# Keys stored in runs for three dilations, strided queries copied by GpSimd, rotary tables made in place

## The chip, the core and the metric

The kernel runs on one core of a Trainium2 chip. The metric is the device time of one execution in microseconds, the median of several runs. The engines run side by side, each through its own queue in order: TensorE (PE; its weight loads are PEld), VectorE (DVE), ScalarE (ACT), GpSimd (POOL), and SyncE (SP), which here only issues DMAs.

## What is computed

A decoder layer on 2048 tokens of 1024 channels: an adaLN-modulated RMS norm, one input projection, then two mixers side by side, a gated linear recurrence (512 channels) and an attention of 8 heads of 64 with rotary queries and keys, and an output projection. What matters here is the attention. It is done three times, with (window, dilation) of (128, 1), (512, 4) and (2048, 16), and the three results are mixed by their softmax denominators:

```python
def dilated_attention(q, k, v, window, dilation):
    L = S // dilation
    blk = window // dilation                       # 128 in all three
    ...                                            # token l * dilation + r goes to residue r, place l
    scores = einsum('bhrnqd,bhrnkd->bhrnqk', qb, kc)   # a block of 128 queries, its own and the previous 128 keys
    scores = where(valid, scores, NEG_INF)
    ...
outs, lses = zip(*[dilated_attention(qh, kh, vh, w, d) for (w, d) in DILATED_PATTERNS])
wts = softmax(stack(lses), axis=0)
att = einsum('pbhs,pbhsd->bhsd', wts, stack(outs))
```

All is float32. The kernel splits each operand of a matmul into a high and a low part and adds three products.

## The kernel before

**First stage.** The tokens go in four chunks of 512. Per chunk: load x (`load_x`), normalise, transpose, modulate into a high and a low part of h (`prep_h`, L301), then the projections. `qk` (L376) multiplies four 128x512 tiles from PSUM by the cosine and sine tables and stores rotated queries and keys, split in two, to DRAM (L395). The tables of a chunk come from `trig` (L238): a DMA broadcasts 512 positions to all partitions into a turn buffer (`half_t` or `rot_t`, which `qk` and `gb` use as well), VectorE reduces the angles, ScalarE takes sines, VectorE finishes into `cos_t`. `v` (L398) scales a value tile by ScalarE, and SP stores it (L406). Weights come through `weights` (L317): DMA, a cast by ScalarE, the low part by GpSimd (L344). The chunks run in two halves (0, 1 and 2, 3); `load(2)` and `load(3)` hold the `trig` of their chunk. In this stage a planner orders the instructions of each engine from its own costs.

**Attention** (`attend`, L1097). Here PE, DVE, ACT and POOL keep the written order; SP's order stays the planner's. Four head pairs, one head in each half of the partitions. `load_pair` brings q and k (high and low, `qs`, `kh`, `kl`), `load_values` the values, one DMA per pattern and chunk. A pair has 19 groups in the order of `SEQUENCE` (L32): 0 is dilation 1, 1 dilation 4, 2 dilation 16. A group has two units of 128 queries by 256 keys, or four units by 128 keys (dilation 16, and the first chunk of dilation 4). Per group: `scores` (L654) issues, for each unit, three products for each of the two heads, the queries as weights and the keys as moving operand, both read with the step of the dilation (`slice(r0, r1, 4)`); VectorE adds the mask and takes the minimum (L670), ScalarE the exponentials (L678); four or five steps later (a step is one head of a group, 38 a pair) `transposed` (L681) and `values` (L696) follow; `evacuate` (L711) writes the result back in token order.

**Mixing the patterns.** Events are counted in steps (`after`, L733). The statistics of a chunk go through DRAM and back (`turn_stats`, `pass_stats`, L755 to L763); `shares` (L765) is called for chunks 0 to 2 at the end of the pair and for chunk 3 some 20 steps into the next, and stores the weights of the patterns (L787). `spread` (L792) reads them back as W, broadcast over 64 partitions, for chunk n of the pair, 7 steps apart; three steps later `combine` (L801) gives GpSimd six operations of 128x512 (L805 to L808), and six steps after that `split_y` (L811) has a copy by VectorE (L815) and a subtraction by GpSimd (L816). So most of this work of a pair falls into the next pair.

**Last stage** (`project`, L1124): the output projection, block by block, the recurrent part ahead of the attention part, the closing norm and the store.

## Time and profile before

| | us |
|---|---|
| three runs | 1185.92, 1184.37, 1180.71 |
| median | 1184.37 |
| the profiled execution | 1180.56 |
| its span, first to last instruction | 1178.8 |

| engine | busy us | share of the span | instructions |
|---|---|---|---|
| PE | 1096.3 | 93% | 6645 |
| DVE | 758.4 | 64% | 1655 |
| ACT | 612.6 | 52% | 1512 |
| POOL | 457.3 | 39% | 297 |

[...] How the views are read: a windows row gives the stretch, its length, the busy us of PE, PEld, DVE, ACT and POOL with their counts, then the granted clock, the DMA engines' busy share and GB/s. A timeline row gives start, duration, engine, line, operation, out<-in and count, and in brackets how long the engine had been idle before it and what it waited for; neighbours of one kind are merged, so matmuls that overlap show a longer time together than they take of the engine, and the distance to the next start is what they cost. A wait row says who waited for whom. DMA-issuing instructions don't count as busy.

### The profile page before, as it was taken

To read this page: it belongs to the slowest core of one execution; us is meant where nothing else is said; L and a number is where in the kernel's file an instruction comes from. 1 tells how busy PE (TensorE), PEld (TensorE's weight loads), DVE (VectorE), ACT (ScalarE), POOL (GpSimd) and SP (SyncE) were. 2 spreads that over 40 slices of the span, in tenths; PEclk is the share of its full clock that TensorE was granted. 3 is DMA by queue.
4 is the path that set the end of the run, shared out by engine and by line. 5 is a ranking of instruction groups with operands and counts; after the bars stand their busy time and mean duration, and the time that the engine had idled before them with its cause. 6 is when DMAs were issued, how large, how long until landed. Compare 5 with 4: busy or idle time off the path is not lost.

```text
span 1178.8 us, 18472 instructions
## 1 busy us (share of the span) xinstructions
PE 1096.3 (93%) x6645; PEld 899.0 (76%) x6645; DVE 758.4 (64%) x1655; ACT 612.6 (52%) x1512; POOL 457.3 (39%) x297
## 2 busy tenths in 40 slices
PE   5868999869989999999999999999999998999996
PEld 2546888768967778888898888878777876778885
DVE  4766497677555645879565266687597783355556
ACT  5544353447547223654545377767678674223332
POOL 1434434234143553436234170083361563742222
PEclk9988999999999999999999999989999989999998
DMA  9533335152253344427222724858659447976654
GB/s 338 191 116 131 116 119 169 60 180 90 85 147 125 110 141 135 124 91 196 82 90 77 227 77 98 179 135 221 164 124 236 127 146 147 269 231 215 186 152 143
DMA packets 164859, 176.49 MB, mean 150 GB/s; under 512 B 25168, under 2 KB 119840, under 8 KB 164768
## 3 DMA queue, kind: packets, MB, share of 16 engines
q1 hardware_dynamic: 164768, 175.32, 51.9%
q8 instruction: 52, 0.85, 0.3%
q14 instruction: 39, 0.32, 0.1%
HBM read 124.49 MB, written 50.79 MB: 149 GB/s over the span
## 4 chain that ended last, share of the span: by engine, by line
PE 52%; DMA 18%; DVE 12%; POOL 7%; issue 5%; ACT 4%; SPq 2%; DVEq 0%; POOLq 0%; ACTq 0%
PE sp L665 5%; DMA st_s<-stat 3%; PE pt L688 3%; DMA wgate<-in_w_ada 3%; DMA W<-f_s 2%; PE pvo L705 2%; PE pv L369 2%; PE pv L370 2%; PE pv L371 2%; PE pmixa L909 2%; POOL W L805 2%; PE pmixb L927 2%; PE pmixa L907 2%; PE pgb L358 2%; PE pgb L357 2%
## 5 line engine op out<-in xcount | busy, mean ns | idle before, releaser
L344 POOL TENSOR_TENSOR wl<-wst,wh 128x1024 fp32r<-128x1024 f32 (+2 forms) x72 | 138.5, 1945 | 203.1 <-ACT wh L342 203.1
L670 DVE CUSTOM_DVE_ANT_0 pm<-sp,table 128x256 f32<-128x256 f32 (+1 forms) x384 | 119.2, 360 | 48.3 <-PE sp L665 42.9
L665 PE MATMUL sp<-kh,qs 64*128 64x256 f32 (+1 forms) x768 | 131.9, 388 | 8.9 <-DVE S L670 5.2
L805 POOL TENSOR_TENSOR W<-W,o 128x512 f32<-128x512 f32 x48 | 60.7, 1294 | 151.0 <-DMA W<-f_s 151.0
L665 PEld LDWEIGHTS sp<-kh,qs 64*128 64x128 f32 x768 | 100.8, 274 | 24.0 <-issue 12.4
L688 PE MATMUL pt<-table,pm 128*128 128x128 f32 x600 | 88.8, 294 | 2.7 <-ACT pT L693 1.5
L705 PE MATMUL pvo<-pT,vt 128*64 128x128 f32 (+1 forms) x1072 | 87.6, 306 | 0.0
L342 ACT CAST wh<-wst 128x1024 fp32r<-128x1024 f32 (+2 forms) x72 | 51.8, 761 | 56.3 <-DMA wst<-in_w_in 26.6
L688 PEld LDWEIGHTS pt<-table,pm 128*128 128x128 f32 x600 | 69.4, 148 | 15.1 <-issue 3.0
L369 PE MATMUL pv<-wh,hh 128*128 128x256 f32 x256 | 72.8, 284 | 7.6 <-ACT vr L404 4.4
L705 PEld LDWEIGHTS pvo<-pT,vt 128*64 128x64 f32 x1072 | 63.4, 144 | 19.2 <-issue 14.4
L370 PE MATMUL pv<-wl,hh 128*128 128x256 f32 x256 | 72.7, 284 | 3.6 <-POOL wl L344 3.6
L952 POOL TENSOR_TENSOR mix<-mix,xt 128x1024 f32<-128x1024 f32 x15 | 36.6, 2441 | 100.1 <-DVE mix L951 60.1
L665 PE MATMUL sp<-kl,qs 64*128 64x256 f32 (+1 forms) x384 | 75.4, 366 | 0.0
L678 ACT ACTIVATE pm<-pm,stat 128x256 f32<-128x256 f32 (+1 forms) x128 | 60.2, 474 | 25.5 <-DVE stat L670 25.5
L371 PE MATMUL pv<-wh,hl 128*128 128x256 f32 x256 | 72.3, 282 | 0.0
L678 ACT ACTIVATE pm<-pm,turn 128x256 f32<-128x256 f32 (+1 forms) x128 | 62.8, 495 | 16.3 <-DVE turn L670 16.3
L357 PE MATMUL pa<-hl,wh 128*128 128x512 f32 x128 | 52.7, 412 | 17.0 <-DVE hl L313 14.7
L691 DVE COPY pT<-pt 128x512 f32<-128x512 f32 (+1 forms) x96 | 63.7, 679 | 0.8 <-PE pt L688 0.5
L665 PEld LDWEIGHTS sp<-kl,qs 64*128 64x128 f32 x384 | 57.8, 277 | 0.0
L437 DVE SCALAR_TENSOR_TENSOR xc<-xr,cols,xc 128x512 f32<-128x512 f32 x48 | 55.5, 1156 | 0.8
L369 PEld LDWEIGHTS pv<-wh,hh 128*128 128x128 f32 x256 | 49.0, 191 | 8.8 <-ACT vr L404 5.1
(275 smaller groups left out, 3131.8 us busy)
## 6 DMA issues: line engine op xcount, KB each, us to landing
wst<-in_w_in SPq DMA_DIRECT2D x32, 512.0 KB
W<-f_s SPq DMA_DIRECT2D x32, 384.0 KB
x_t<-in_x SPq DMA_DIRECT2D x16, 512.0 KB
wada<-in_w_ada SPq DMA_DIRECT2D x16, 512.0 KB
wst<-in_w_in SPq DMA_DIRECT2D x32, 256.0 KB
vt<-v_s SPq DMA_DIRECT2D x32, 256.0 KB
yat<-y_s SPq DMA_DIRECT2D x32, 256.0 KB
yb_s<-yb SPq DMA_DIRECT2D x16, 512.0 KB
```

What stands on the lines that cost most here:

```text
L344: nc.gpsimd.tensor_tensor(lo, i, hi.bitcast(F32), ALU.subtract)
L357: nc.tensor.matmul(o, lhsT=wh[:, k, sl], rhs=hl[:, k, :], start=False, stop=False)
L369: nc.tensor.matmul(o[:, 0:256], lhsT=hh[:, k, sl], rhs=wh[:, k, :], start=k == 0, stop=False)
L370: nc.tensor.matmul(o[:, 0:256], lhsT=hh[:, k, sl], rhs=wl[:, k, :], start=False, stop=False)
L371: nc.tensor.matmul(o[:, 0:256], lhsT=hl[:, k, sl], rhs=wh[:, k, :], start=False, stop=k == KC - 1)
L665: nc.tensor.matmul(self.sp[h][:, o:o + n], lhsT=x[rows, q], rhs=y[rows, k], start=j == 0, stop=j == 2)
L670: v.tensor_tensor_reduce(out=pm[:, o:o + n], in0=sp[:, o:o + n], in1=self.mask[:, 256 - n:256], scale=-0.125, scalar=3e38, op0=ALU.add, op ...
L678: nc.scalar.activation(pm[:, o:o + n], pm[:, o:o + n], AF.Exp, bias=self.stat(ctx, s, b), scale=-1.0, accum_out=self.stat(ctx, 2 + s, b))
L688: nc.tensor.transpose(pt[:, k * P:(k + 1) * P], pm[:, k * P:(k + 1) * P], self.ident)
L691: nc.vector.tensor_copy(pT[:, 0:tot], pt[:, 0:tot])
L705: self.mark = nc.tensor.matmul(self.bank[p][64 * s:64 * s + 64, o:o + w], lhsT=ctx["vt"][p, b][:, s], rhs=ctx["pT"][:, c:c + w], start=fir ...
L805: e.tensor_tensor(W[:, p], W[:, p], self.o.pop((pr, p, n)), ALU.mult)
```

## The change

- Keys: within a chunk of 512, token 16 i + r is stored at place 32 r + i. `qk` does this in its four products for K, reading PSUM and the tables with a step of 16 elements and writing in a row. The scores then read the keys of any dilation in runs (8 elements for dilation 1, 32 for 4 and 16). A dilation-1 unit of 256 keys that spans two chunks becomes two matmuls of 128 columns per product.
- The masks of dilation 1 and 4 get the same order (`masks`, two VectorE copies), and so do the values: their loads for dilation 1 and 4 are four DMAs instead of one.
- Queries of dilation 4 and 16 are copied side by side by GpSimd (`queries`: two copies of 128x512 per chunk or four units, 16 a pair), issued two groups ahead (`AHEADQ`), into two buffers that take the place of `cos_t`. Dilation-1 queries are read as before.
- `trig` works in the table itself, and its position DMA writes there: for chunks 0 and 1 before the modulation's weights are loaded, for 2 and 3 right before `trig`.
- The value stores are issued by ScalarE instead of SP.
- The six operations of `combine` are given to GpSimd as four one step later and two another step later.

```diff
+AHEADQ = 2
...
+    def masks(self, pool):
+        self.masked = [pool.tile([P, 2 * P], F32, name=f"mask{r}") for r in (16, 4)] + [self.mask]
+        for r, m in zip((16, 4), self.masked):
+            self.nc.vector.tensor_copy(m.rearrange("p (two r i) -> p two r i", two=2, r=r),
+                                       self.mask.rearrange("p (two i r) -> p two r i", two=2, r=r))
...
+    def load_positions(self, c):
+        pi = self.cos_t[:, 2 * (c % 2) + 1, :].bitcast(I32)
+        self.nc.sync.dma_start(pi, self.io["positions"][:, c * CH:(c + 1) * CH].to_broadcast([P, CH]))
     def trig(self, c):
-        rot = self.turn()
-        pi = rot[:, 0, :].bitcast(I32)
-        nc.sync.dma_start(pi, self.io["positions"][:, c * CH:(c + 1) * CH].to_broadcast([P, CH]))
...
+        cos, sin = (self.cos_t[:, 2 * (c % 2) + n, :] for n in range(2))
+        v.tensor_copy(sin, sin.bitcast(I32))
...
     def qk(...)
+        def times(to, x, y):
+            if which == "k":
+                to = to.rearrange("p (r i) -> p r i", r=16)
+                x, y = (t.rearrange("p (i r) -> p r i", r=16) for t in (x, y))
+            nc.vector.tensor_tensor(to, x, y, ALU.mult)
...
     def v(...)
-            nc.sync.dma_start(self.v_s[r0:r0 + P, 4 * quad:4 * quad + 4, :], vr)
+            nc.scalar.dma_start(self.v_s[r0:r0 + P, 4 * quad:4 * quad + 4, :], vr)
...
     def load_values(...)
+        elif p == 1:
+            for m in range(4):
+                self.nc.sync.dma_start(flat[32 * m:32 * m + 32],
+                                       vs.rearrange("(i m r) e -> m i r e", m=4, r=4)[m])
+        else:
+            for b in range(4):
+                self.nc.sync.dma_start(flat[:, b], vs[P * b:P * b + P].rearrange("(i r) e -> r i e", r=16))
...
+    def keys(x, p, blocks):
+        c, j = divmod(blocks[0], 4)
+        if p == 2:
+            return [(x.rearrange("p (c r i) -> p r c i", c=4, r=16)[:, blocks[0]], 0, P)]
+        if p == 1:
+            n = len(blocks)
+            x = x[:, c * CH:(c + n) * CH].rearrange("p (c m r i) -> p r c m i", c=n, m=4, r=4)
+            return [(x[:, j], 0, n * P)]
+        x = [x[:, c * CH:c * CH + CH].rearrange("p (r b i) -> p b r i", r=16, b=4) for c in (c, c + (j == 3)) if c < 4]
+        if len(blocks) == 1 or j < 3:
+            n = len(blocks)
+            return [(x[0][:, j:j + n], 0, n * P)]
+        return [(x[0][:, 3], 0, P), (x[1][:, 0], P, P)]
+    def queries(self, p, n):
+        self.copies = (self.copies + 1) % 2
+        q = self.qc[self.copies]
+        x = self.qs.rearrange("p k (i r) -> p k r i", r=16)[:, :, 4 * n:4 * n + 4] if p == 2 else (
+            self.qs[:, :, n * CH:n * CH + CH].rearrange("p k (i r) -> p k r i", r=4))
+        for k in range(2):
+            self.nc.gpsimd.tensor_copy(q[:, k], x[:, k].bitcast(F32))
+        return q
...
     in source(), attention()
+                    copy_queries(pr, i + AHEADQ)
...
     def combine(...)
+        for i in range(3):
+            self.after(i, lambda some=ops[2 * i:2 * i + 2]: [e.tensor_tensor(*op) for op in some])
         self.after(SPLIT, lambda: self.split_y(cb, gb, pr, n))
```

## Rows read from the trace of the kernel before

**Rows 1.** Windows by stage: the first stage, then the four head pairs of the attention.

```profile
0.00:667.70 667.70, 612.39 (x3013) 498.13 (x3013) 429.04 (x557) 322.65 (x533) 251.68 (x152) 0.97 0.42 134
667.70:736.70 69.00, 68.56 (x651) 57.97 (x650) 47.61 (x218) 52.61 (x204) 26.20 (x18) 0.95 0.46 122
736.70:814.90 78.20, 75.51 (x709) 63.45 (x708) 58.72 (x244) 56.70 (x215) 35.26 (x28) 0.93 0.76 174
814.90:893.40 78.50, 74.67 (x709) 62.91 (x708) 59.58 (x244) 56.59 (x215) 35.14 (x28) 0.96 0.70 165
893.40:973.60 80.20, 75.58 (x710) 63.16 (x710) 61.49 (x248) 56.98 (x214) 35.18 (x28) 0.94 0.59 163
```

**Rows 2.** Timeline, VectorE and TensorE: stands in the first stage.

```profile
93.07 0.43 DVE L245 CAST half_t<-half_t 128x512 f32<-128x512 int32 x1 [12.21 <-DMA half_t<-in_positions]
...
94.15 0.80 PE L357 MATMUL pa<-hl,wh 128*128 128x512 f32 x1 [11.74 <-DVE hl L313]
...
218.27 0.43 DVE L245 CAST rot_t<-rot_t 128x512 f32<-128x512 int32 x1 [10.84 <-DMA rot_t<-in_positions]
...
346.66 0.43 DVE L245 CAST half_t<-half_t 128x512 f32<-128x512 int32 x1 [3.92 <-DMA half_t<-in_positions]
```

**Rows 3.** Windows: two stretches of the first stage.

```profile
200.00:270.00 70.00, 57.15 (x312) 48.87 (x311) 48.69 (x60) 34.09 (x55) 22.47 (x12) 0.93 0.36 113
340.00:370.00 30.00, 22.83 (x112) 18.48 (x112) 19.24 (x28) 15.27 (x21) 6.68 (x4) 0.89 0.25 76
```

**Rows 4.** Waits, ScalarE's and SP's: us in total, times, longest.

```profile
ACT vr L404 <- DMA v_s<-vr: 24.1, 6, 8.5
...
SPq L763 <- DMA st_s<-stat: 69.2, 14, 8.8
```

**Rows 5.** Timeline, TensorE: scores of dilation 16, 4 and 1, each with what follows.

```profile
781.02 0.48 PE L665 MATMUL sp<-kh,qs 64*128 64x128 f32 x2
...
783.81 1.09 PE L688 MATMUL pt<-table,pm 128*128 128x128 f32 x8
...
785.86 0.61 PE L665 MATMUL sp<-kh,qs 64*128 64x256 f32 x2
...
787.58 1.09 PE L688 MATMUL pt<-table,pm 128*128 128x128 f32 x8
...
801.26 0.39 PE L665 MATMUL sp<-kh,qs 64*128 64x256 f32 x2
...
802.16 1.09 PE L688 MATMUL pt<-table,pm 128*128 128x128 f32 x8
```

**Rows 6.** Timeline, TensorE: the first 128-key scores of dilation 1.

```profile
667.90 0.27 PE L665 MATMUL sp<-kl,qs 64*128 64x128 f32 x2
668.01 0.44 PE L665 MATMUL sp<-kh,qs 64*128 64x128 f32 x4
```

**Rows 7.** Single lines of the kernel: duration in ns, minimum, median, maximum.

```profile
L855 POOL CAST wo<-wo_st x6: 609/610/1038, 676.5 to 698.7; 128x512 fp32r<-128x512 f32 x4, 128x1024 fp32r<-128x1024 f32 x2
...
L730 DVE COPY o<-pvo x24: 673/1055/1154, 682.6 to 966.0; 128x512 f32<-128x512 f32 x24
...
L890 DVE TENSOR_REDUCE ysq<-fsq x16: 1018/1078/1097, 1013.2 to 1159.2; 128x128 f32<-128x512 f32 x16
...
L781 DVE TENSOR_TENSOR sd<-sw,S x8: 234/249/1245, 743.4 to 985.5; 96x96 f32<-96x96 f32 x4, 32x96 f32<-32x96 f32 x4
...
L406 SPq DMA_DIRECT2D v_s<-vr x32: 319/320/564, 252.3 to 625.6; - x32
```

**Rows 8.** Timeline, SP's queue: two loads of W in the third head pair.

```profile
833.62 1.26 SPq L796 DMA_DIRECT2D W<-f_s  x2
```

**Rows 9.** Timeline, GpSimd and VectorE: the first weighted sum of that pair.

```profile
843.41 3.74 POOL L805 TENSOR_TENSOR W<-W,o 128x512 f32<-128x512 f32 x3 [31.24 <-DMA W<-f_s]
...
849.80 1.26 POOL L808 TENSOR_TENSOR gbt<-W,gbt 128x512 f32<-128x512 f32 x1
...
851.10 0.43 DVE L815 CAST yb<-gbt 128x512 fp32r<-128x512 f32 x1 [7.35 <-POOL gbt L808]
```

More of the change, by code (lines that the diff above doesn't have):

```diff
@@ L588, in attention, with copy_queries @@
             values_of(0, 1, n)
+        order = [list(self.groups(p)) for p in range(3)]
+        order = [(p, order[p][SEQUENCE[:i].count(p)]) for i, p in enumerate(SEQUENCE)]
+        opens = [p and g[2] for p, g in order]
+        copies = {}
+        def copy_queries(pr, i):
+            if i >= len(order):
+                pr, i = pr + 1, i - len(order)
+            if pr < 4 and opens[i]:
+                p, n = order[i][0], order[i][1][4]
+                copies[pr, p, n] = self.queries(p, n)
         def source():
+            for i in range(AHEADQ):
+                copy_queries(0, i)
             for pr in range(4):
@@ L594, in source @@
                 stat = [turn, cb.tile([P, 4, 16], F32, name="stat1"), S[:, 2]]
-                groups = [self.groups(p) for p in range(3)]
                 left = [SEQUENCE.count(p) for p in range(3)]
-                for i, p in enumerate(SEQUENCE):
-                    g = next(groups[p])
+                for i, (p, g) in enumerate(order):
                     left[p] -= 1
                     n = g[4]
+                    copy_queries(pr, i + AHEADQ)
                     for s in range(2):
-                        yield {"pr": pr, "p": p, "s": s, "g": g, "vt": vts[pr], "stat": stat[p], "S": S}
+                        yield {"pr": pr, "p": p, "s": s, "g": g, "vt": vts[pr], "stat": stat[p], "S": S,
+                               "q": copies.get((pr, p, n))}
                     if pr < 3:
@@ L660, in scores @@
             self.sp = [ps.tile([P, 512], F32, name="sp", tag="mm") for _ in range(2)]
-            for b, q, k, n, o in units:
-                for j, (x, y) in enumerate(((self.qh, self.kh), (self.qh, self.kl), (self.ql, self.kh))):
-                    for h in range(2):
-                        rows = slice(64 * h, 64 * h + 64)
-                        nc.tensor.matmul(self.sp[h][:, o:o + n], lhsT=x[rows, q], rhs=y[rows, k],
-                                         start=j == 0, stop=j == 2)
+            terms = (0, self.kh), (0, self.kl), (1, self.kh)
+            for b, blocks, n, o in units:
+                heads = [slice(64 * h, 64 * h + 64) for h in range(2)]
+                qs = [[ctx["q"][rows, x, b % 4] if p else self.qs[rows, x, P * b:P * b + P] for x in range(2)]
+                      for rows in heads]
+                ks = [[self.keys(y[rows], p, blocks) for _, y in terms] for rows in heads]
+                for part, (_, at, w) in enumerate(ks[0][0]):
+                    for j, (x, _) in enumerate(terms):
+                        for h in range(2):
+                            nc.tensor.matmul(self.sp[h][:, o + at:o + at + w], lhsT=qs[h][x], rhs=ks[h][j][part][0],
+                                             start=j == 0, stop=j == 2)
         sp = self.sp[s]
         pm = wk.tile([P, 512], F32, name="pm", bufs=PMB)
-        for b, q, k, n, o in units:
-            v.tensor_tensor_reduce(out=pm[:, o:o + n], in0=sp[:, o:o + n], in1=self.mask[:, 256 - n:256],
+        for b, _, n, o in units:
+            v.tensor_tensor_reduce(out=pm[:, o:o + n], in0=sp[:, o:o + n], in1=self.masked[p][:, 256 - n:256],
                                    scale=-0.125, scalar=3e38, op0=ALU.add, op1=ALU.min, accum_out=self.stat(ctx, s, b))
@@ L676, in exponentials @@
         s, pm = ctx["s"], ctx["pm"]
[L677 removed]
+        for b, _, n, o in ctx["g"][0]:
             nc.scalar.activation(pm[:, o:o + n], pm[:, o:o + n], AF.Exp, bias=self.stat(ctx, s, b), scale=-1.0,
@@ L1026, in run @@
                     ws = [h1p.tile([P, 4, 2, 512], F32, name="wada", tag=t) for t in ("s1h", "s1l")]
+                    for c in range(2):
+                        self.load_positions(c)
                     self.ada_half(ws, reca, "ri", ps, ld, 0)
@@ L1104, in attend @@
             ps = Banks((psm, 2), (psa, 2))
-            qs = sh.tile([P, 2, T], F32R, name="qs", tag="t1")
-            self.qh, self.ql = (qs[:, s] for s in range(2))
+            self.qs = sh.tile([P, 2, T], F32R, name="qs", tag="t1")
+            qc = sh.tile([P, 2, 2, 4, P], F32R, name="qc", tag="t0")
+            self.qc, self.copies = [qc[:, n] for n in range(2)], 0
             self.kh, self.kl = (sh.tile([P, T], F32R, name=n, tag=t) for n, t in (("kh", "t3"), ("kl", "t4")))
```

64 lines of the change are left out of this document (29 added, 35 removed).

## Prediction

> **What bounds the kernel now.** I read the stages first. Before the first score the core spends 667.7 us, in which TensorE is busy 612.4; the four head pairs of the attention take 69.0, 78.2, 78.5 and 80.2 us, TensorE busy in 68.6, 75.5, 74.7 and 75.6 of them [rows 1]. (The borders are the first score of each pair.) So TensorE sets the pace nearly everywhere, and a gain needs either less time per matmul or the removal of one of its stands. VectorE (59 to 61 us a pair) and ScalarE (57) are not far behind, GpSimd (35) is [rows 1].
>
> In the first stage the long stands begin with VectorE in front of the angle work of a chunk: it waits 12.21, 10.84 and 3.92 us for the positions, and all that is queued behind waits too. After the first, TensorE has stood 11.74 us for a half of h that VectorE owed it [rows 2]. The second lies in 200 to 270 us, in which TensorE is busy 57.15 of 70 at a mean granted clock of 0.93; the third in 340 to 370, 22.83 of 30 at 0.89 [rows 3]. ScalarE also waited 24.1 us, six times, for a value store to leave its buffer [rows 4].
>
> In the attention a group is scores, then transposes, then values. A dilation-16 group starts at 781.02 and its scores end at 783.81: 2.79; the transposes and values take until 785.86: 2.05. The dilation-4 group after it takes 1.72 for the scores of two 256-key units; a dilation-1 group with the same 256-key units takes 0.90 (801.26 to 802.16) [rows 5]. The strided operands cost the difference. Whole groups, scores plus 2.05: 2.95, 3.77 and 4.84.
>
> **What the change does, part by part.**
>
> *Scores.* Each of the four head pairs has 8 dilation-1 groups, 6 of dilation 4 with 256 keys, and 5 with four 128-key units. The six fall from 1.72 to 0.90: 4.9 us. In the five, 12 pairs of matmuls (one per half of the array) start every 0.11 us when nothing is strided (668.01 less 667.90 [rows 6]); with the 0.24 that the 0.90 has beyond six such steps that is 1.56 instead of 2.79: 6.2 us for five. Against that, three dilation-1 units now lie in two chunks and take six steps instead of three, 0.9 us. Together 10.2 us a pair. That keys in runs of 8 or 32 read as fast as contiguous ones is not shown in the trace; the bounds are the 0.90 and the 1.72 of [rows 5], and I take 0.90, since the weights (the queries) become contiguous in any case.
>
> [...] A step of 4 is exactly dilation 4, and 1.72 against 0.90 says that it is not free here. [...]
>
> *First stage.* The positions go to the table itself, free much earlier, and those of chunks 0 and 1 are loaded ahead of the modulation's weights. The first stand goes: 12.2 us of VectorE, less the K products of chunk 0, which now read at a step of 64 bytes. VectorE rows bound a strided 128x512: 0.67 contiguous, 1.055 with a strided write, 1.08 with a strided read [rows 7]; I take 1.06, four times 0.39, so 1.6 us; net 10.5 on the path. For chunk 2 the table is free once K of chunk 0 is multiplied; I keep 3 of the 10.84 us. Of TensorE's 12.85 idle us there I take 11 as won, because the value stores, which caused the last of them, leave SP too (32 issues of 0.32 us [rows 7], now on ScalarE, where the next tile's scaling queues behind them; it has room, 323 of 668 busy [rows 1]). Third stand: VectorE's 3.92 and what follows at a lowered clock, 5.5. The two early position loads go ahead of the weights of the modulation: 1 us lost (bounds 0 and two issues of 0.63, as W's [rows 8]). The other 28 slower K products and two mask copies hide under TensorE, which is the busiest there by far (612 against VectorE's 429 [rows 1]); without that cover they would cost 12 us. Sum: -26.
>
> *Query copies.* 64 copies of 128x512 by GpSimd, 16 a pair, each from a step of 16 or 64 bytes. Bounds: 0.61, its contiguous cast, and 2.0, its product of two operands (1.26 [rows 9]) lengthened as VectorE's write is, 1.57 times. I take 0.61 x 1.57 = 0.96, being nearest to a copy. They add 15 us a pair to 35. What matters is where they stand: GpSimd runs in program order. The copies for a group are issued two groups ahead, and from the second pair on GpSimd also has the weighted sums of the pair before. The first of them waits for W by DMA: it starts at 843.41, 28.5 us after its pair (814.9), having idled 31.24; two more pairs show the same [rows 9]. W is late because SP has stood for the statistics (69.2 us in 14 waits [rows 4]) and sends W at 833.62, 18.7 into the pair [rows 8]. That is latency, not TensorE's pace, so I leave it at 28.5 (0 to 6 us more if the value loads, four issues instead of one, come in front).
>
> Counting the steps of the source (groups numbered from 0): the first sum, six operations (L805 to L808), lies after the copies of group 6 and before those of group 8. Group 8 would start at 25 us now (4 x 2.95 + 2 x 3.6 + 2 x 2.95), but its copies come after W and six operations: 28.5 + 7.7 + 1.9 = 38.1. From there GpSimd has, in order, the y split 1.3, a sum 7.7, two groups' copies, split 1.3, a sum in two pieces with a group's copies between, split 1.3, four operations 5.1 and the copies of group 17: with the first sum 32.1 us besides ten copies. The last groups then take 5.9. A pair is so 28.5 + 32.1 + 10 x 0.96 + 5.9 = 76.1 us, against 78.2, 78.5 and 80.2 now, and not the 61 that the matmuls allow. Today VectorE waits there too (7.35 us for the same sum [rows 9]), so much of the old stall is in both. A stand of 13 us also lowers the clock (the stretches with stands show 0.93 and 0.89 [rows 3]), 2 us a pair. Left of 8.6 us: 3 for the three pairs. In the first pair there are no sums; it gains 8 of the 10.2, ScalarE having 52.6 us of work in it [rows 1].
>
> VectorE's small operations with two SBUF inputs take 0.25 us, but up to 1.25 in some places [rows 7]. [...]
>
> *Last stage.* Sums in three pieces come a step or two later; TensorE has other blocks to project. 0, bounds -3 and +5.
>
> **Sum** against the profiled execution, 1180.6 (span 1178.8): -26 -8 -3 = 1143.6. The median of the runs lies 3.8 above it, so 1147.
>
> **The rivals.**
> 1. *The copies don't wait* (SP sends W earlier, or VectorE's stall was the larger share): pairs 1 to 3 keep their present stall of 7 us over 61, 68 us each, 30 better: 1117. For it: W's place in SP's order is a planner's. Against: two statistics round trips stand before it in all three pairs. 0.15.
> 2. *The matmuls gain nothing*, the keys' runs being as slow as strides: pair 0 stays, the others take 38.1 + 42 = 80 and the 2 of the clock: 1164. 0.07.
> 3. *The first stage gives little*: VectorE's order is the planner's, and the next late thing (weights by GpSimd, ScalarE's tables) takes the place; 8 instead of 26: 1165. 0.13.
> 4. *Slower*: GpSimd becomes the bound through the copies. A pair is 66.5 + 10c for a copy of c us; all other gains (34) are spent when three pairs are 11.3 longer than today, at c = 2.4. At 2.6 each pair is 92.5: some 1191. For it: nothing shows GpSimd reading at a step. Against: 0.61 contiguous. 0.10.
>
> **How the numbers follow.** Forecast 0.55, 1147, its own range 1130 to 1165. Bounds: copies of 0.61 give 10 less, of 2.0 give 31 more; W 6 us later, 18 more. Range 1110 to 1178, leaving out most of rival 4 and the tails. About 0.5% (6 us) is what a measurement of this kernel tells from no change. Faster 0.83 (rivals 1 to 3 and most of the forecast), same 0.07, slower 0.10.
>
> **What would show it.** Score parts of 0.9 and 1.5 us; no wait of VectorE for positions over 4 us; copies near 1 us; in pairs 1 to 3 a stand of TensorE at group 8, ended by a copy, with the sum just before it on GpSimd. Wrong, if the pairs last under 70 us (copies don't wait) or over 82, or if the first stage ends after 655.

## The result: 1200.28 us, 1.4% slower

The changed kernel takes 1200.28 us, the median of 4 runs (1199.35 to 1201.0), beside 1183.53 for the kernel before (1180.71 to 1185.92, 4 runs): a ratio of 1.0142, with an interval of 1.0117 to 1.0167. The profiled execution has a span of 1198.8 us against 1178.8. The prediction said 1147 and faster; it was wrong in size and in sign.

First the windows of the changed kernel by stage, which answer to [rows 1]. The columns are the stretch, its length, busy time of TensorE, of its weight loads, of VectorE, ScalarE and GpSimd (with instructions), mean granted clock, DMA share and GB/s. The stretches are the first stage, the four head pairs and the rest; the last pair is counted here to the last matmul on the values, which makes it 87.0 us in the kernel before.

```profile
0.00:649.80 649.80, 608.41 (x3015) 495.34 (x3015) 443.43 (x559) 320.92 (x532) 253.89 (x156) 0.99 0.42 135
649.80:721.00 71.20, 57.53 (x667) 47.28 (x666) 48.54 (x225) 52.51 (x206) 40.84 (x32) 0.93 0.53 139
721.00:813.00 92.00, 71.17 (x728) 58.15 (x728) 59.65 (x238) 55.79 (x211) 51.82 (x44) 0.83 0.67 151
813.00:904.20 91.20, 72.08 (x727) 59.39 (x726) 59.91 (x244) 57.26 (x217) 51.72 (x44) 0.83 0.70 152
904.20:996.90 92.70, 73.61 (x794) 59.61 (x793) 68.10 (x263) 62.86 (x228) 49.69 (x42) 0.89 0.51 136
996.90:1198.80 201.90, 183.92 (x796) 149.06 (x794) 93.51 (x130) 61.23 (x120) 74.26 (x43) 0.96 0.68 191
```

Against the kernel before, the first stage gives 17.9 us back, pair 0 costs 2.3, pairs 1 to 3 cost 32.2 together (275.9 against 78.2 + 78.5 + 87.0) and the rest 3.4. That is the 20.0 us between the two spans. TensorE's busy time in pair 1 fell, from 75.5 to 71.2 us, but the pair is 13.8 us longer, because TensorE now stands in it for 20.8 us, and runs at a mean granted clock of 0.83 of full speed where it had 0.93. Cut into windows of 1 us, the pair shows 1.00 in 57 of them, 0.50 in 28 and values between in 7, so (1 - 0.83) x 2 x 92 = 31 of the 92 us lie at half clock, against 11 of 78 before.

The faster scores are there. The next lines are of TensorE's timeline in the changed kernel (start, duration, line, operation, tiles, shapes, count): the scores of a dilation-1, a dilation-16 and a dilation-4 group, each with the transposes that end it. They take 0.91, 1.48 and 0.93 us, where [rows 5] had 0.90, 2.79 and 1.72.

```profile
691.13 0.38 PE L733 MATMUL sp<-kh,qs 64*128 64x256 f32 x2
...
692.04 1.09 PE L756 MATMUL pt<-table,pm 128*128 128x128 f32 x8
...
694.09 0.33 PE L733 MATMUL sp<-kh,qc 64*128 64x128 f32 x2
...
695.57 1.09 PE L756 MATMUL pt<-table,pm 128*128 128x128 f32 x8
...
697.62 0.39 PE L733 MATMUL sp<-kh,qc 64*128 64x256 f32 x2
...
698.55 1.09 PE L756 MATMUL pt<-table,pm 128*128 128x128 f32 x8
```

(Dilation 1 reads the queries qs where they lie, the others the copies qc.) What TensorE waits for stands on the page, in the costliest groups: 56.4 of the 64.4 us idle before the scores that read copies were ended by a query copy.

```profile
L733 PE MATMUL sp<-kh,qc 64*128 64x128 f32 (+1 forms) x512 | 65.2, 320 | 64.4 <-POOL qc L616 56.4
```

The largest of these stands in pair 1, in two timelines. GpSimd gets to the first weighted sum at 751.20, 30.2 us into the pair, and to the copies for group 8 behind it at 758.75; TensorE, with group 8 next, has stood 8.83 us when the first copy is done. These lines answer to [rows 9], where the same sum stood 28.5 us into its pair and nothing of TensorE's was queued behind it.

```profile
751.20 3.70 POOL L875 TENSOR_TENSOR W<-W,o 128x512 f32<-128x512 f32 x3 [7.60 <-DVE pT L759]
754.86 2.60 POOL L875 TENSOR_TENSOR W<-W 128x512 f32<-128x512 f32 x2
757.54 1.26 POOL L875 TENSOR_TENSOR gbt<-W,gbt 128x512 f32<-128x512 f32 x1
758.75 2.24 POOL L616 CAST qc<-qs 128x512 fp32r<-128x512 f32 x2
```

```profile
759.83 0.47 PE L733 MATMUL sp<-kh,qc 64*128 64x128 f32 x2 [8.83 <-POOL qc L616]
```

The first row puts GpSimd's wait down to a VectorE copy (pT) that the sum doesn't read. By the trace's semaphore times the last piece of W landed at 751.04, 0.16 us before the sum, so W is what came late here too. Pairs 2 and 3 have the same stand with 9.42 and 9.81 us; there the wait before the sum is put down to W itself (9.57 and 8.39 us).

### The profile page after: what moved, and what is told of

The parts are those of the page before. It is cut to its first block, busy times and chain, and to the rows that moved or that the text cites. A ratio compares the mean times of both kernels' runs of the same rounds, so it can differ in the third digit from the quotient of the medians.

```text
span 1198.8 us, 18814 instructions
## 1 busy us (share of the span) xinstructions
PE 1066.7 (89%) x6717; PEld 868.8 (72%) x6717; DVE 773.1 (64%) x1657; ACT 610.6 (51%) x1511; POOL 522.2 (44%) x361
## 4 chain that ended last, share of the span: by engine, by line
PE 54%; DMA 14%; POOL 12%; DVE 10%; ACT 4%; issue 4%; SPq 2%; DVEq 0%; POOLq 0%; ACTq 0%
POOL W L875 5%; DMA W<-f_s 5%; PE sp L733 4%; PE pt L756 3%; PE pvo L773 3%; PE pv L378 3%; PE pv L379 3%; PE pv L377 3%; PE pgb L366 2%; PE pgb L364 2%; PE pgb L365 2%; DMA wgate<-in_w_ada 2%; POOL qc L616 2%; DMA f_s<-sw 2%; PE pa L365 2%
## 5 line engine op out<-in xcount | busy, mean ns | idle before, releaser
L733 PE MATMUL sp<-kh,qc 64*128 64x128 f32 (+1 forms) x512 | 65.2, 320 | 64.4 <-POOL qc L616 56.4
L738 DVE CUSTOM_DVE_ANT_0 pm<-sp,mask 128x256 f32<-128x256 f32 (+1 forms) x256 | 91.2, 397 | 47.6 <-PE sp L733 46.0
L733 PEld LDWEIGHTS sp<-kh,qc 64*128 64x128 f32 x512 | 49.1, 211 | 75.5 <-POOL qc L616 60.6
L616 POOL CAST qc<-qs 128x512 fp32r<-128x512 f32 x64 | 70.4, 1133 | 60.3 <-DMA qs<-q_s 51.1
L756 PE MATMUL pt<-table,pm 128*128 128x128 f32 x600 | 92.4, 301 | 4.7 <-ACT pT L761 3.5
L756 PEld LDWEIGHTS pt<-table,pm 128*128 128x128 f32 x600 | 72.1, 153 | 15.9 <-ACT pT L761 4.7
L761 ACT COPY pT<-pt 128x512 f32<-128x512 f32 (+1 forms) x56 | 31.8, 568 | 53.5 <-PE pt L756 53.4
L746 ACT ACTIVATE pm<-pm,S 128x128 f32<-128x128 f32 x128 | 49.8, 392 | 12.9 <-DVE S L738 12.1
L974 PE MATMUL pmixa<-wo,yat 128*128 128x512 f32 x128 | 51.4, 402 | 4.6 <-DMA yat<-y_s 4.6
```

Of the source, the lines that this page charges most:

```text
L616: self.nc.gpsimd.tensor_copy(q[:, k], x[:, k].bitcast(F32))
L733: nc.tensor.matmul(self.sp[h][:, o + at:o + at + w], lhsT=qs[h][x], rhs=ks[h][j][part][0], start=j == 0, stop=j == 2)
L738: v.tensor_tensor_reduce(out=pm[:, o:o + n], in0=sp[:, o:o + n], in1=self.masked[p][:, 256 - n:256], scale=-0.125, scalar=3e38, op0=ALU.ad ...
L746: nc.scalar.activation(pm[:, o:o + n], pm[:, o:o + n], AF.Exp, bias=self.stat(ctx, s, b), scale=-1.0, accum_out=self.stat(ctx, 2 + s, b))
L756: nc.tensor.transpose(pt[:, k * P:(k + 1) * P], pm[:, k * P:(k + 1) * P], self.ident)
```

## The experiments

Every run is measured beside the kernel before on the same chip (its medians were 1187.33 for e1 to e4, 1187.22 for e5 to e8 and 1185.01 for e9 to e11). The stages of the profiled executions, in us, with borders as above:

| run | median | first stage | pair 0 | 1 | 2 | 3 | rest |
|---|---|---|---|---|---|---|---|
| before | 1183.53 | 667.7 | 68.9 | 78.2 | 78.5 | 87.0 | 198.5 |
| changed | 1200.28 | 649.8 | 71.2 | 92.0 | 91.2 | 92.7 | 201.9 |
| e1 first stage only | 1167.64 | 653.1 | 71.5 | 80.1 | 81.7 | 85.2 | 201.7 |
| e2 sums 3 steps later | 1175.95 | 651.5 | 70.2 | 75.1 | 81.2 | 89.6 | 207.1 |
| e3 no copies | 1184.14 | 649.2 | 70.3 | 81.4 | 87.1 | 92.9 | 200.8 |
| e4 strided queries read | 1175.55 | 651.2 | 69.6 | 81.7 | 81.7 | 90.0 | 201.4 |
| e5 keys in token order | 1185.30 | 652.9 | 59.7 | 93.3 | 85.6 | 89.7 | 202.1 |
| e6 sum and split later | 1190.27 | 651.6 | 58.8 | 79.9 | 90.1 | 103.9 | 201.6 |
| e7 e5 and e6 | 1186.39 | 652.6 | 59.3 | 81.7 | 90.9 | 102.9 | 199.2 |
| e8 one value load | 1186.83 | 651.8 | 58.1 | 92.8 | 88.8 | 91.5 | 202.3 |
| e9 chain's end later | 1165.35 | 652.4 | 61.4 | 74.9 | 80.6 | 92.1 | 208.2 |
| e10 e9, keys in token order | 1155.11 | 646.4 | 59.5 | 73.0 | 74.6 | 87.5 | 206.4 |
| e11 e1 and e9 | 1174.19 | 650.9 | 68.9 | 75.8 | 77.3 | 100.7 | 200.2 |

The first stage is nearly the same program in e1 to e11 (the K products, the masks and the first query copies differ), and still lies between 646.4 and 653.1: a difference of a few us between two profiles says nothing by itself. A profiled execution can also lie some us from its run's median: e1's took 1175.07 us, e9's 1171.3, e10's 1149.2.

**e1: the first stage's part of the change alone.** The kernel before with tables in place, early positions and value stores by ScalarE.

```diff
+                    for c in range(2):
+                        self.load_positions(c)
...
-            nc.sync.dma_start(self.v_s[r0:r0 + P, 4 * quad:4 * quad + 4, :], vr)
+            nc.scalar.dma_start(self.v_s[r0:r0 + P, 4 * quad:4 * quad + 4, :], vr)
```

> The kernel before with the first stage's part alone: positions into the tables, loaded ahead, and value stores by ScalarE; K's order, scores, copies and sums as before. In the changed kernel the first score came 18.0 us earlier (649.8 instead of 667.7). Theory 'order' (the attention loses because the query copies stand behind other work on GpSimd): the gain stays whole here, 1166 +- 3, and attention pairs of 78 us as before. Rival 'shift' (the attention only pays later what the first stage gained, because loads and sums are tied to time and not to TensorE): 1175 or more, with the pairs some 3 us longer each.

Measured: 1167.64 us, a ratio of 0.9843 (0.9799 to 0.9887). So this part is worth some 19 us by itself (13 to 24 by the interval), and what the attention's part adds to it is a loss of 33 to 36, as one compares the medians or the ratios. The median fits the "order" theory. The profiled execution, at 1175.07 the longest of the four, has pairs 0 to 2 some 2 to 3 us longer than before, as "shift" had them; a small part of that kind isn't ruled out.

**e2: the sums three steps later.**

```diff
-        self.after(3, lambda: self.combine(cb, W, gb, pr, n))
+        self.after(6, lambda: self.combine(cb, W, gb, pr, n))
```

> The changed kernel with one number altered: the weighted sums of GpSimd are issued six steps after the load of W instead of three, so that all the query copies of groups 8, 11, 12, 14 and 17 stand ahead of the sum that they stood behind. The amount of work on every engine is the same. Theory 'order': TensorE's stands on copies in pairs 1 to 3 (9.4, 6.1 us and the like, with the half clock after them) go, the pairs fall from 92 to 72 to 76 us, total 1145 to 1160. Rival 'sum' (VectorE has to wait for the late sum in any case, so TensorE stands there instead): pairs 85 or more, total 1185 or more. Rival 'load' (GpSimd has too much work or disturbs the others, in whichever order): 1195 to 1200.

Measured: 1175.95, a ratio of 0.9913 (0.9878 to 0.9948). This is between the theories. Moving nothing but the place of the sum in GpSimd's list takes 24 us off the changed kernel, so standing behind the sum did cost the copies time. But the time did not reach 1145 to 1160. In pair 2 TensorE stands again, for VectorE's copy of the transposed weights; VectorE had waited for the sum, and the sum for W, 38.6 us into the pair (lines of VectorE, GpSimd, TensorE).

```profile
843.11 0.43 DVE L882 CAST yb<-gbt 128x512 fp32r<-128x512 f32 x1 [5.88 <-POOL gbt L875]
```

```profile
835.40 3.77 POOL L875 TENSOR_TENSOR W<-W,o 128x512 f32<-128x512 f32 x3 [10.38 <-DMA W<-f_s]
```

```profile
844.97 1.94 PE L756 MATMUL pt<-table,pm 128*128 128x128 f32 x8 [5.44 <-DVE pT L759]
```

**e3: no copies after the first pair.** The later pairs' strided groups score with queries left from the first pair, so the scores of dilation 4 and 16 there are not the right ones; no time of any other operation is left out.

```diff
-        for k in range(2):
+        for k in range(2 if pr == 0 else 0):
             self.nc.gpsimd.tensor_copy(q[:, k], x[:, k].bitcast(F32))
```

> The changed kernel, but the queries of dilation 4 and 16 are copied in the first pair only; later pairs read what lies in the buffers, so this part of the computation is left out. TensorE's operands keep their form. Theory 'order': pairs 1 to 3 at 70 to 75, some 1145 to 1155, like the kernel with later sums. Rival 'sum': 85 or more a pair, 1185 or more, since VectorE's wait for the sum (7.8 to 8.7 us in each of these pairs) stays and TensorE stands for it. Rival 'load': under 70 a pair, 1130 to 1140, clearly faster than the kernel with later sums.

Measured: 1184.14, a ratio of 0.9979 (0.9943 to 1.0014). With no copy in the way the scores' gain still doesn't arrive; the rival was nearly right. The wait sits one engine further on: in pair 2 W lands 36.8 us into the pair, VectorE stands 16.38 us in front of its rounding of y (L882, issued six steps after the sum), and TensorE 13.84 us for a mask that is queued behind.

```profile
845.32 0.43 DVE L882 CAST yb<-gbt 128x512 fp32r<-128x512 f32 x1 [16.38 <-POOL gbt L875]
```

```profile
846.49 0.47 PE L733 MATMUL sp<-kh,qs 64*128 64x128 f32 x1 [13.84 <-DVE stat L738]
```

**e4: keys in runs, but the strided queries read directly.**

```diff
-        for k in range(2):
-            self.nc.gpsimd.tensor_copy(q[:, k], x[:, k].bitcast(F32))
-        return q
+        return x
```

> The changed kernel without copies: the queries of dilation 4 and 16 are read with their step as before, the keys in runs. Theory 'order', with contiguous weights as the source of the faster scores: score parts return to 1.7 (dilation 4) and 2.6 to 2.8 us (four units), no stand on a copy, pairs near 78, total 1165 to 1172 (the first stage's 18 us remain). Rival 'keys' (the keys' runs are what made the scores fast): 0.9 and 1.5 us as with copies, pairs near 68 to 72, total 1140 to 1150.

**e5: queries copied, but keys, masks and value loads as before.**

```diff
-            return [(x.rearrange("p (c r i) -> p r c i", c=4, r=16)[:, blocks[0]], 0, P)]
+            return [(x.rearrange("p (i r) -> p r i", r=16)[:, blocks[0]], 0, P)]
...
-            x = x[:, c * CH:(c + n) * CH].rearrange("p (c m r i) -> p r c m i", c=n, m=4, r=4)
-            return [(x[:, j], 0, n * P)]
+            return [(x[:, c * CH:(c + n) * CH].rearrange("p (i r) -> p r i", r=4)[:, j], 0, n * P)]
```

> The changed kernel with the keys, the masks and the value loads of the kernel before (keys in token order, one value load in place of four); only the queries are copied side by side, and the rest of the change stays. Run e4 read strided queries against keys in runs and had 1.62 and 2.77 us for the score parts of dilation 4 and 16, nearly those of before. Theory 'queries alone' (it is the strided queries, loaded as weights, that were slow): the parts stay at 0.91 and 1.5 us here, the keys' order and its fourfold value loads bought nothing. Rival 'both': the parts go back to 1.7 and 2.8. On the time: if the 4x value loads in SP's queue make the weights W late, the pairs fall from 92 to 85 or less and the whole to 1180 or less; if the queue has nothing to do with it, the whole stays within 5 us of the changed kernel's 1200.

Measured: e4 1175.55 (0.9906, 0.9868 to 0.9944), e5 1185.3 (0.9979, 0.9957 to 1.0001). The two belong together, for the score parts. TensorE's timeline of e4, dilation 4 and dilation 16:

```profile
671.40 0.51 PE L731 MATMUL sp<-kh,qs 64*128 64x256 f32 x2
...
673.02 1.09 PE L754 MATMUL pt<-table,pm 128*128 128x128 f32 x8
...
678.73 0.43 PE L731 MATMUL sp<-kh,qs 64*128 64x128 f32 x2
...
681.50 1.09 PE L754 MATMUL pt<-table,pm 128*128 128x128 f32 x8
```

and of e5, dilation 16 and dilation 4:

```profile
684.68 0.36 PE L710 MATMUL sp<-kh,qc 64*128 64x128 f32 x2
...
686.19 1.09 PE L733 MATMUL pt<-table,pm 128*128 128x128 f32 x8
...
688.24 0.48 PE L710 MATMUL sp<-kh,qc 64*128 64x256 f32 x2
...
689.81 1.09 PE L733 MATMUL pt<-table,pm 128*128 128x128 f32 x8
```

| score part, us | keys strided | keys in runs |
|---|---|---|
| queries strided, dilation 4 | 1.72 [rows 5] | 1.62 |
| queries copied, dilation 4 | 1.57 | 0.93 |
| queries strided, dilation 16 | 2.79 [rows 5] | 2.77 |
| queries copied, dilation 16 | 1.51 | 1.48 |

In the 128-key units of dilation 16 the strided weights alone were slow, and the keys' order buys nothing. In the 256-key units of dilation 4 either stride is enough to keep them slow, and only both edits together help. So neither theory of e5 was right for both patterns.

On the time, e5 fits neither bound. Pair 0 takes 59.7 in place of 71.2 us, pair 1 is as long as in the changed kernel (93.3). The first sum starts 30.6, 24.7 and 23.4 us into pairs 1 to 3, against 30.2, 29.0 and 26.4 there: the value loads make W a little late in two of three pairs, and it is not much that this costs. Most of what e5 gains is pair 0, and e8 says why. e4's score parts are those of "order", and its time lies 4 us above the 1172 that went with them. Without a copy it has 82, 82 and 90 us for pairs 1 to 3, but not by e3's stands: TensorE is busy for 77.9, 77.4 and 87.1 of them and stands longer than 1.5 us only once (3.11), while VectorE waits 6.8, 8.5 and 5.7 us for the first sum. Under the old scores most of that wait is covered; in e3, with the short ones, TensorE stands 7.65, 13.84 and 8.56 us for it.

**e6: the sum two steps and the split two more steps later, for three pairs; the first pair's output weights 10 steps later on GpSimd.**

```diff
-        self.after(3, lambda: self.combine(cb, W, gb, pr, n))
+        self.after(5 if pr < 3 else 3, lambda: self.combine(cb, W, gb, pr, n))
...
-        self.after(SPLIT, lambda: self.split_y(cb, gb, pr, n))
+        self.after(8 if pr < 3 else SPLIT, lambda: self.split_y(cb, gb, pr, n))
...
-                    if i >= WO_FIRST and (i - WO_FIRST) % WO_STEP < 3:
+                    if i == WO_FIRST or i >= WO_FIRST + 10 and (i - WO_FIRST) % WO_STEP < 3:
```

> The changed kernel with, for the first three pairs, the sum begun 5 steps after W's load is issued in place of 3, and VectorE's split of the sum 8 steps after it in place of 6; the output weights of pair 0 begin 10 steps later on GpSimd. Theory 'order of issue' (the stands come from copies and splits that are issued a fixed number of steps after a load whose landing is bound to time, not to steps): pair 0 loses its 10 us stand, pairs 1 to 3 fall from 92 to 73 to 78, half clock to some 10 us a pair, the whole 1145 to 1160. Rival 'pair loads' (TensorE then catches up with the loads of the next pair's keys and queries, which SP issues at fixed steps too): the stands move to the start of the pair and to the last sums, pairs 80 to 85, the whole 1170 to 1180, as in e2.

**e7: e5 and e6 in one.**

> e5 and e6 together: keys in token order with single value loads, queries copied, sums and splits later, output weights of pair 0 later. Theory 'order of issue plus SP's queue': nothing is left of the stands but a few us, pairs 72 to 75, the whole 1135 to 1150, better than e6 by 5 us or more. Rival: SP's queue is not what makes the loads late, and the whole is that of e6 within 5 us. If the scores need the keys in runs (rival 'both' of e5), the pairs go back to 78 or more and the whole to 1165 or more.

Measured: e6 1190.27 (1.0021, 0.9997 to 1.0045), e7 1186.39 (0.9994, 0.9971 to 1.0018). For e6 both theories missed; e7 is that of e6 within 5 us, as its rival had it. VectorE no longer waits for the sum in the pairs of either, and pair 0 takes 59 us; but the other stand is back. In e6's pair 1, GpSimd waits for W until 740.46, 30 us into the pair, and the copies that TensorE needs next are issued between two pieces of the sum:

```profile
740.46 3.71 POOL L875 TENSOR_TENSOR W<-W,o 128x512 f32<-128x512 f32 x3 [7.06 <-DMA W<-f_s]
744.14 1.25 POOL L875 TENSOR_TENSOR W<-W 128x512 f32<-128x512 f32 x1
745.35 2.01 POOL L616 CAST qc<-qs 128x512 fp32r<-128x512 f32 x2
```

```profile
746.42 0.48 PE L733 MATMUL sp<-kh,qc 64*128 64x128 f32 x2 [5.79 <-POOL qc L616]
```

Two steps are some 4 us, and W is later than that: a sum issued two steps later still waits, now with another group's copies behind it.

**e8: one DMA for each value tile of dilation 1 and 4 in place of four.** The values then don't lie in the order of the keys, so the sums take the wrong rows; no work but the DMA issues is left out.

```diff
+        self.nc.sync.dma_start(flat, vs.rearrange("(i r) e -> i r e" if p else "(r i) e -> i r e", i=P))
-        if p == 2:
...
-            for b in range(4):
-                self.nc.sync.dma_start(flat[:, b], vs[P * b:P * b + P].rearrange("(i r) e -> r i e", r=16))
```

> The changed kernel with one DMA in place of four for each value tile of dilation 1 and 4; the rows of the values then don't stand in the order of the keys, so the values that are summed are the wrong ones, and nothing else differs. If SP's 24 extra issues a pair delay the chain from the statistics to W, W lands near 28 us into the pair in place of 30 to 39, and the whole falls to 1180 or less; if not, it stays at 1195 to 1205.

Measured: 1186.83 (0.9987, 0.997 to 1.0004), 13 us below the changed kernel, and in the profiles nearly all of it in pair 0: 58.1 against 71.2. It is not W that does this: the first sum starts 30.7, 24.8 and 24.4 us into pairs 1 to 3, and they keep their 89 to 93 us. In pair 0 GpSimd's copies are queued behind the first scaling of the output weights. In the changed kernel that one waits for its load until 667.65, and the next copies are issued at 673.97:

```profile
667.65 2.85 POOL L920 TENSOR_SCALAR wo_st<-wo_st,cols 128x1024 f32<-128x1024 f32 x1 [47.02 <-DMA wo_st<-in_w_out]
...
673.97 2.12 POOL L616 CAST qc<-qs 128x512 fp32r<-128x512 f32 x2
```

```profile
675.10 0.58 PE L733 MATMUL sp<-kh,qc 64*128 64x256 f32 x2 [10.66 <-POOL qc L616]
```

In e8 the same operation starts at 656.68 and TensorE doesn't stand:

```profile
656.68 2.85 POOL L912 TENSOR_SCALAR wo_st<-wo_st,cols 128x1024 f32<-128x1024 f32 x1 [34.01 <-DMA wo_st<-in_w_out]
```

SP issues the output weights' loads behind the first values' loads. With four issues a tile it comes to them at 662.97, with one at 651.90.

**e9: the end of the chain later as a whole.** For three pairs W's loads are issued 7 steps later, the sum 5 steps behind them (3) and the split 7 behind the sum (6); the output weights as in e6.

```diff
-            self.after(3 + PACE * (n - a), lambda n=n: self.spread(...))
+            self.after((10 if pr < 3 else 3) + PACE * (n - a), lambda n=n: self.spread(...))
-        self.after(3, lambda: self.combine(cb, W, gb, pr, n))
+        self.after(5 if pr < 3 else 3, lambda: self.combine(cb, W, gb, pr, n))
-        self.after(SPLIT, lambda: self.split_y(cb, gb, pr, n))
+        self.after(7 if pr < 3 else SPLIT, lambda: self.split_y(cb, gb, pr, n))
```

> The changed kernel with the end of the chain of the first three pairs moved later as a whole, not stretched: W's loads are issued 7 steps later, the sum 5 steps after them (3), the split 7 after the sum's beginning (6), so that the first sum of a pair is issued in step 18 of 38 of the next pair, behind the copies for the group at which TensorE stood and past the moment at which W landed in e5 (23 to 31 us); the output weights of pair 0 begin 10 steps later on GpSimd. Theory 'order of issue' (each engine takes its work in order, the chain's end is bound to time, TensorE's groups to steps): without a wait in front of copies and splits each pair runs as pair 0 does where nothing is in its way (58 to 60 us in e5, e6 and e8), at most as long as VectorE's 61 us of work in a pair: pairs 1 to 3 60 to 70, the whole 1105 to 1135. Rival 'pair loads': the loads of the next pair's keys, queries and values and the statistics' round trips can't follow that pace; the stands come back at other engines and the pairs stay at 78 to 90, the whole 1165 to 1190.

**e10: e9 with keys in token order**, as in e5, and the output weights where the changed kernel has them. Against e5 three numbers differ.

> e9 with the keys in token order and single value loads, as in e5 (the output weights of pair 0 where they were). Score parts of dilation 4 at 1.57 in place of 0.91 us cost some 6 x 0.66 = 4 us a pair of TensorE's time, the value loads of e9 cost SP 24 more issues a pair. By 'order of issue' alone: 0 to 12 us above e9. If SP's queue is what is left in e9, it is below e9 by 5 us or more.

**e11: e1 with the chain moved as in e9.**

> e1 (the first stage's part of the change alone: scores, keys and queries as before) with the chain of the first three pairs moved later as in e9. By 'order of issue' the old kernel's pairs had the same wait, only shorter: pairs 1 to 3 fall from 80, 82, 85 to the 71 of pair 0, or to 72 to 76, the whole to 1140 to 1155, and the difference between this run and e9 is then what the faster scores are worth when nothing stands in their way (some 20 to 40 us). Rival: the old pairs are bound by TensorE's own 75 us of work, they stay at 78 to 82, and the whole at 1160 to 1170.

Measured: e9 1165.35 (0.9827, 0.9805 to 0.9849), e10 1155.11 (0.9738, 0.9712 to 0.9765), e11 1174.19 (0.9911, 0.9896 to 0.9926). The windows of e10's four pairs:

```profile
646.40:705.90 59.50, 58.75 (x649) 47.12 (x648) 47.26 (x218) 52.24 (x204) 41.20 (x32) 1.00 0.51 137
705.90:778.90 73.00, 67.55 (x709) 54.04 (x708) 55.95 (x242) 56.13 (x215) 39.49 (x34) 0.95 0.79 162
778.90:853.50 74.60, 67.31 (x711) 54.07 (x710) 62.18 (x244) 56.54 (x216) 52.26 (x45) 0.95 0.82 183
853.50:941.00 87.50, 76.53 (x774) 60.55 (x773) 69.44 (x262) 60.61 (x226) 58.38 (x50) 0.92 0.61 140
```

e10 is the fastest of all that ran, 30 us below the kernel before and 45 below the changed one; some 19 of the 30 are the first stage's (e1). That profiled execution (span 1147.4) was among its shortest. Every engine does the same work in e10 as in e5, which takes 1185.3: the 30 us between them (28 by the ratios) are the order of issue alone, and the granted clock comes back with it, from 0.85 in e5's pair 1 to 0.95. In pair 1 of e10, GpSimd copies queries at 738.77 and starts the first sum behind them, 34.9 us into the pair, with no wait: W is there.

```profile
738.77 2.09 POOL L593 CAST qc<-qs 128x512 fp32r<-128x512 f32 x2 [6.49 <-PE sp L710]
740.82 3.78 POOL L852 TENSOR_TENSOR W<-W,o 128x512 f32<-128x512 f32 x3
```

"Order of issue" holds for pairs 1 and 2 and not for the sizes: it had 60 to 70 us a pair and 1105 to 1135. The rival holds in part; e9's time lies at the lower end of its 1165 to 1190. In e9, TensorE begins pairs 1 to 3 with single waits of up to 5.4, 4.8 and 3.6 us for their keys; at the same place e10, with fewer issues on SP, has none above 1.3. e10 is 10 us below e9, the outcome that was named for SP's queue; e9 itself, with the whole change, is only about as fast as e1. In pairs 2 and 3 of e10 the first sum waits for W again (5.0 and 1.3 us) and copies are waited for still, 2.3 and 3.7 us. And pair 3 and the rest, 293.9 us, are no better than in e5 (291.8).

e11 has the kernel before's scores with the same late chain, and both its theories missed (1140 to 1155, 1160 to 1170): it is 7 us slower than e1, which has no late chain. Its pairs 1 and 2 fall to 75.8 and 77.3 us, TensorE 74.6 and 75.9 busy, so there is next to no stand left in them; its pair 3 takes 100.7 where e1 had 85.2. Near the end of that pair ScalarE stands for the load of the output weights, and TensorE for ScalarE's copy of transposed weights behind it (lines of ScalarE and TensorE):

```profile
965.28 1.15 ACT L847 ACTIVATE wo<-wo_st,cols 128x1024 fp32r<-128x1024 f32 x1 [6.83 <-DMA wo_st<-in_w_out]
```

```profile
967.93 1.12 PE L687 MATMUL pt<-table,pm 128*128 128x128 f32 x4 [6.69 <-ACT pT L692]
```

SP could issue that load at 958.99 only, having stood 7.1 us for a product of the last sum of pair 2: the load goes into buffers that held attention results which the sums read. So a later chain also lets go of its buffers later. e6 and e7, whose pair 3 is as long, stand at the same place for 8.44 and 6.99 us.

e10's median is 19.1 us below e11's; the profiled spans differ by 26.4, of which 4.5 lie in the first stage, where both do nearly the same. What copied queries are worth when the chain is out of their way is 9.4 us in pair 0, and 2.8 and 2.7 in pairs 1 and 2, where TensorE is busy 7.1 and 8.5 us less but loses a part to stands again. The rest is pair 3, 13.2 us shorter, less a last stage that is 6.2 longer.

## Why the prediction was wrong

Set against the prediction's sum, the profiled execution is 57 us longer: the first stage 8, pair 0 10, pairs 1 to 3 35, the rest 3. Of its own signs, the score parts, the positions, the copies and the stand at group 8 came as named; pairs of 91 to 93 us are the one that it gave for being wrong.

**Right: the scores.** 0.9 and 1.5 us were forecast, 0.93 and 1.48 came. Pair 0 without a stand (e8, 58.1, against 68.9) gains even more than the 8 forecast. That the weights' order is what matters was only half of it, as e4 and e5 show: for dilation 4 it takes the keys' runs too. With strided keys or strided queries, at a step of 4 fp32, the part takes 1.57 or 1.62 us in place of 0.93.

**Right: where GpSimd would be late.** The first sum at 28.5 us of the pair, the copies done at 38.1: they came at 30.2 and 40.0 in pair 1, with TensorE standing at group 8. A copy took 1.09 us (median of 64; 1.03 to 1.59) and not 0.96; over ten copies this is 1.3 us a pair.

**Wrong: what follows that point.** The formula of a pair, 28.5 + 32.1 + 10c + 5.9, takes GpSimd's list from the first sum on as if it ran without a gap. From 761.0 to the end of pair 1 it has 38.0 us (the 32.1 less the first sum's 7.7, eight copies of 0.96, and 5.9); there are 52, and GpSimd is busy in 37.9 of them:

```profile
761.00:813.00 52.00, 42.20 (x432) 34.83 (x432) 37.27 (x138) 31.87 (x120) 37.89 (x32) 0.84 0.64 147
```

The 14 us that the formula lacks are what the pair is longer than the 78 that it gave with the clock's 2. Of them 12.6 are three waits of GpSimd in its turn, ahead of the copies for group 17; what follows those copies took 7.2 us and not 5.9.

```profile
777.26 1.29 POOL L883 TENSOR_TENSOR yb<-gbt,yb 128x512 fp32r<-128x512 f32 x1 [3.23 <-DVE yb L882]
...
792.72 1.29 POOL L883 TENSOR_TENSOR yb<-gbt,yb 128x512 fp32r<-128x512 f32 x1 [4.60 <-DVE yb L882]
798.80 3.71 POOL L875 TENSOR_TENSOR W<-W,o 128x512 f32<-128x512 f32 x3 [4.79 <-DMA W<-f_s]
802.47 1.26 POOL L875 TENSOR_TENSOR W<-W 128x512 f32<-128x512 f32 x1
803.68 2.11 POOL L616 CAST qc<-qs 128x512 fp32r<-128x512 f32 x2
```

VectorE's rounding of y (L882) is issued six steps after its sum, and stands in VectorE's list behind masks and copies for TensorE's groups. VectorE was not idle meanwhile: before the two roundings it was busy in 2.70 of 2.73 and 3.52 of 4.12 us of GpSimd's wait. So GpSimd waits there for its place in another engine's list, and TensorE for GpSimd's copies. The fourth sum waits for its own W, whose statistics are taken up only some 20 steps into the pair; the copies of group 17 are behind it, and TensorE stands 5.90 us more. The prediction counted the order of the lists on GpSimd alone, and never asked which of its operations wait for another engine's place in another list. e3 shows the VectorE side of it without the copies and e2 with copies that stand ahead, e6 the copies without the VectorE side. In e9 and e10, with the chain later, no stand of TensorE for a copy in pairs 1 and 2 is above 2.8 us, and VectorE no longer waits for the sum in them; the first sum itself still waits for W, 6.6 and 5.4 us in e9, 0 and 5.0 in e10.

**Wrong: the clock.** 2 us a pair were taken from the stretches of [rows 3]. The granted clock in pairs 1 and 2 is 0.83, after stands of 2.7 to 9.4 us, two or three a pair; 20 us more of pair 1 lie at half clock than before. With that, TensorE's busy time in pair 1 fell by 4.3 us and not by 10.2. In these pairs it went with the stands: in e9, which has the same scores but no stand of that size on a copy, pair 1 has 0.93 and TensorE is busy 64.6 us; in e10, with slower dilation-4 scores, 0.95 and 67.6. That stands alone lower it is not shown: pair 0 of e1 has 0.90, with TensorE busy in 71.1 of its 71.5 us.

**Wrong: pair 0.** "There are no sums in it" was true, and overlooked what else is in GpSimd's list: the scaling of the output weights, which waits for a load. The prediction did name the fourfold value loads as something that could come in front of W, with 0 to 6 us; it did not look for what else stands behind them on SP. They cost 13 us, nearly all of it there (e8).

**Half right: the first stage.** 18 of the 26 us came. Of VectorE's waits for the positions one of 0.5 us is left; the angle work of chunks 0 and 1 now starts at 12 us. Set matmul by matmul against the trace of before, the same matmul starts 6.3 us later at 82 us, 6.8 earlier at 100, 2.0 later at 240, 11.0 earlier at 281, 19.8 at 372 and 18.0 at 417 and after. So the first stand gave 6.8 net of what went ahead of it, the second 4.2 and the third 8.8, and 1.8 were lost behind, in place of 9.5, 11 and 5.5. The first term is short by what goes ahead: matmuls of the modulation that started at 43.42 in the kernel before start at 48.40, TensorE standing 2.75 us for VectorE, which is busy for 44.4 of the first 60 us where it was for 37.8; the prediction had 1 us for all this. Then another load ends late: VectorE waits for the input gate's weights, and TensorE for a block of x behind that.

```profile
77.59 0.43 DVE L164 CAST w_rg_x_h<-w_rg_x_st 128x512 fp32r<-128x512 f32 x1 [7.54 <-DMA w_rg_x_st<-in_w_rg_x]
```

```profile
80.64 1.12 PE L306 MATMUL xT<-table,x_t 128*128 128x128 f32 x4 [7.12 <-DVE x_t L319]
```

The second is short because new stands took the place of old ones. Three are gone, of 3.25, 1.42 and 4.38 us (TensorE had waited for xc, xh and a value tile vr). But TensorE now stands 2.12 us at 206 for VectorE's products of K, which are queued behind the angle work of chunk 2 and take 1.0 us each in place of 0.68, so these did not all hide under TensorE; it stands 3.10 us at 231 for ScalarE's split of the projection's weights, and 3.57 at 235 for GpSimd's, which had cost 2.55 and 1.09. Whether the early position loads push the gate's weights back was not tried by itself and stays open.

**The rivals.** Rival 4 had the place of the loss (GpSimd in front of TensorE) and nearly its size (92.5 us a pair), but as a price of the copies, at 2.6 us each. They cost 1.09, and in e3, without them, the pairs are still 81, 87 and 93 us, so its nearness in size is luck. Rival 3 was right in less than half of its amount: 8 us of the first stage's gain stayed out, where it had 18. Rival 2's 1164 leaves out the 3.8 us from the profile to the median (1180.6 - 26 + 9.1 + 3.8 is 1167.5); nothing else hangs on that. The "slower" end should not have hung on the price of one operation, but on how many lists with waits in them TensorE had come to depend on.

## What to carry to other kernels

Before an operation is put on an engine that runs in order, list what stands ahead of it there and what each of those waits for, on every engine down the line, and take an engine's work as back to back only where none of it waits for another. A chain that is bound to time (statistics out and in by DMA) but issued by a count of steps moves closer to its waits with every us that the steps get faster: with a faster inner loop the offsets have to be set anew, here to about the landing of W (e5 against e10, 30 us for three numbers). But a chain moved later also keeps its buffers longer, and what loads into them comes late (pair 3 of e11, where ScalarE stands 6.83 us for such a load). One DMA split in four took four places in SP's queue here, and the price, 13 us against e8, was paid by what was queued behind it.

## What the runs showed of the hardware

A strided copy of 128x512 on GpSimd takes 1.09 us (median of 64), where [rows 7] had 0.61 for a contiguous one: 1.8 times.

VectorE's small operations on two operands of SBUF were slow beside those copies. In the changed kernel four copies are on GpSimd from 769.78 on (4.25 us); VectorE's operations of 32x32 and 32x96 in that time take about as long as a copy, 0.82 to 1.09 us each, where [rows 7] had a median of 0.25 us for a like operation.

```profile
769.78 4.25 POOL L616 CAST qc<-qs 128x512 fp32r<-128x512 f32 x4
```

```profile
771.11 0.82 DVE L839 TENSOR_TENSOR sm<-S 32x32 f32<-32x32 f32 x1
771.96 1.07 DVE L840 TENSOR_TENSOR sm<-sm,S 32x32 f32<-32x32 f32 x1
773.06 1.09 DVE L841 TENSOR_TENSOR sw<-sm,S 32x96 f32<-32x96 f32 x1
```

The prediction's sum has no term for such operations. At 0.25 us each the three would take 0.75 us; they took 2.98, so 2.2 us of VectorE went there. What makes them slow was not shown, and no run shows it on TensorE's path by itself.
